# Delta rule of eight samples in a hybrid decoder step: the four heads of a group next to each other on TensorE

## The chip, the cores and the metric

The kernel is one launch on one NeuronCore of a Trainium2 chip. The metric is the device time of an execution in microseconds (us). Below, PE is TensorE, DVE VectorE, ACT ScalarE, POOL GpSimd, and SP the engine that only issues DMAs. A matmul of f32 data is two instructions in the trace, since the engine makes two passes over the moving operand; "pass" means one of these.

## The reference, cut to what matters

One layer of a decoder for a prompt of 512 tokens and for eight samples with one new token each: a modulated norm, an input projection, three branches (RG-LRU, gated DeltaNet, latent attention), their merge, and a feed forward part. What the change touches is the DeltaNet step of the samples. With T = 1 the chunked rule comes down, for each of 8 samples and 8 heads, to:

```python
kS = k @ S                      # S [128, 128], the state of this sample and head
U = beta * (v - exp(g) * kS)
o = exp(g) * (q @ S) + (q . k) * U
S_new = exp(g) * S + outer(k, U)
```

## The kernel before, in words

The kernel runs on one core, in stages: modulation and first norm, input projections with the prompt's delta rule, then a stage in which three things are interleaved (from about 490 to 745 us of the trace): the RG-LRU (`lru_steps`), the delta rule of the samples (`delta_samples`), and steps of the samples' latent attention (`sample_part`), which reads 32 pages of cache per sample. After it come the prompt's attention, the merge of the branches and the feed forward part. A loop over `lru_steps` draws one step of each other generator per turn; the instructions of a turn are then ordered per engine by a scheduler, from which each engine has one fixed list that it works off in order. So an instruction that waits holds up all that stand behind it on its engine.

The tile names that matter:

- `mm<-hh,whi`, `hl,whi`, `hh,wlo` (L170): the large products, each of three exact parts, with weights `raw` loaded from DRAM (L149, issued by ACT's queue), split into `whi` by ACT (L156) and `wlo` by DVE (L157).
- `s` (L871): the RG-LRU's gate products, of `xc` (a convolution, last step L376 on DVE) split into `xch` by ACT (L177) and `xcl` by DVE (L178).
- `sp<-cc,Qst` (L1090) and `sa<-cv,PT` (L1114): scores and weighted values of the latent attention of four samples. The stationary operand has 32 columns, and the outputs of the four samples lie on PSUM partitions 0, 32, 64 and 96, the four of them innermost in the loop. Their pages come by DMA, `cc` from SP (L1068) and POOL (L1063), `cv` from POOL (L1104).
- `St`: the states, eight tiles [128, 512] per group of four heads (four samples each), loaded by SP (L954), updated by DVE (L1011) and written back by SP (L1019).

`delta_samples` works on two groups t of four heads j. Per group PE computes into two PSUM tiles, `pK` and `pV`, with head j on partitions 32 j to 32 j + 7, one row per sample:

- `pK` (L964): for each head, for queries and keys (w = 0, 1), the sum over the samples s of a product whose stationary operand is `msk`, 8 columns of which all but column s are zero, and whose moving operand is the state of that sample and head, 128 columns. That is 64 matmuls, 128 passes, with the heads outermost: all 16 of head 0, then those of head 1, and so on.
- `pV` (L969 to L973): per head five small products that turn values, keys, q . k, exp(g) and -beta to rows per sample: two with 128 moving columns, three with one column.

Then ACT copies `pV` to `vt` (L976, L977), and DVE makes updates and outputs of `vt` and `pK` (L983 to L987). Before the groups, eight matmuls (L943), one per head, spread exp(g) over all partitions.

Of the kernel before, what the change touches and what calls it, by code (L numbers as in the profile page):

```python
# [20 lines left out]
T = 512  # L21
NS = 8
HB = 260          # columns of one half: 256 prompt tokens, then 4 samples
NT = 2 * HB
CW = 544          # columns after a convolution: 8 samples at 4s, prompt token t at 32 + t
# [7 lines left out]
# columns of the parameter array  # L33
# [8 lines left out]
# columns of the constant array  # L42
# [10 lines left out]
# gates whose product starts with the first tiles of the normalised input  # L53
EARLY = 2
# steps of the samples' attention per gate, block of the prompt's attention, part of a merge, step of the RG-LRU,
# block of values, pair of heads
STEPS = (1, 0.9, 1, 0.9, 0.5, 1.5)
# pages of a block of eight that GpSimd fetches; tiles of values
POOLED = (1, 3, 5)
VBUF = 5  # L60
# delta rule of the samples: its start among the steps of the RG-LRU; steps per gate there
DL = 8
GL = 5
# gates after each pair of heads of the delta rule, and before the first
# [7 lines left out]
def pr(t):  # L72
    """prompt columns of a [p, 520] tile"""
    return view2(t)[:, :, 0:256]


def sm(t):
    """sample columns of a [p, 520] tile"""
    return view2(t)[:, :, 256:260]


def csm(t):
    """sample columns of a [p, 544] tile as [p, 2, 4]"""
    return t[:, 0:32].rearrange("p (a b c) -> p a b c", a=2, b=4)[:, :, :, 0]


def cpr(t):
    """prompt columns of a [p, 544] tile as [p, 2, 256]"""
    return t[:, 32:544].rearrange("p (a b) -> p a b", a=2)
# [11 lines left out]
def emit(es, tc, I, O):  # L101
# [23 lines left out]
    e1 = C("eps")[:, 0:1]       # EPS  # L125
    e2 = C("eps")[:, 1:2]       # 4 EPS
    zero1 = C("eps")[:, 3:4]

    # banks of PSUM: the phase's pool, and how many buffers each tag has there
# [22 lines left out]
    def split(raw, n, p=wp, bufs=2):  # L152
        """exact sum of two float32r parts"""
# [9 lines left out]
    def gemm(pt, ws, xs, nk, k0=0, start=True, stop=True, halves=((0, 1),), ks=None):  # L163
        """pt [128, 2, 512] += W^T X over nk k-tiles; ws = (hi, lo), xs = lists (hi, lo) of tiles"""
# [16 lines left out]
    # ---------------------------------------------------------------- modulation and first norm  # L181
# [10 lines left out]
    def ada_a(i, p, bufs):  # L192
        """tiles i and 8 + i of 128 features of the modulation: four quarters of the product"""
# [12 lines left out]
    def ada_b(i, md):  # L206
        """their sum, features on partitions"""
# [6 lines left out]
    def ada_steps(p, bufs):  # L214
        """32 further tiles by eight: four at a time next to each other, two turned by one transposition"""
# [21 lines left out]
    def rstd_a(ss, n, a, p, tiles=None):  # L237
        """1 / sqrt(mean over n features + EPS) of half a from ss, sums of n / 128 squares; tokens on partitions"""
# [9 lines left out]
    def rstd_b(r, rs, pinned=False):  # L248
        """the same on all partitions (PSUM)"""
# [40 lines left out]
    # kept until the branches are merged  # L290
    ckv_s = cp.tile([128, 2, 8], F32, name="ckv_s")
    # latent and rotary rows of queries and new keys of the samples in three tiles of 96
    kns = cp.tile([96, 3, 8], F32, name="kns")
    Qst = cp.tile([96, 3, 8, 32], F32, name="Qst")         # sample, 8 heads and zeros
    G3 = cp.tile([128, 3, 8, 8], F32, name="G3")           # q, k, v of the samples (doubled)
    zz_s = cp.tile([128, 8, 8], F32, name="zz_s")          # z silu(z) of the samples (doubled)
    egS = cp.tile([8, 2, 8], F32, name="egS")              # exp(g), -beta of the samples: sample, head
    gng = cp.tile([128, 1], F32, name="gng")
    V.tensor_scalar(gng, Pm("gng"), 0.5, None, ALU.mult)
    osf = cp.tile([128, 8, 8], F32, name="osf")            # gated delta output of the samples  # L300
    omS = cp.tile([128, 8, 8], F32, name="omS")            # attention output of the samples
# [8 lines left out]
    with ExitStack() as pha:  # L310
# [51 lines left out]
        def conv(p, pt, state, w, bias, nb, y):  # L362
            """causal convolution of width 4 of [128, 2, 260] in PSUM; y: output [128, 544]"""
# [15 lines left out]
        with ExitStack() as sub:  # L379
# [8 lines left out]

            lc = cp.tile([128, 2, 10], F32, name="lc")    # -c/2, c/4 with c = 8 softplus(-lambda)
            R = pa.tile([8, 512], F32, name="R")          # g of the prompt, cumulated within chunks, by head  # L390
            gb = pa.tile([128, 4, 2, 8], F32, name="gb")  # the same and beta; tokens on partitions
            eg = pa.tile([128, 2, 4, 8], F32, name="eg")  # exp(g), -exp(g)

            # ------------------------------------------------------------ scalars of the gated delta rule, rotary key
            def softplus(x, t):
                """max(x, 0) + log1p(exp(-|x|)), log1p(y) = 2 atanh(y / (2 + y)); t: 3 scratch, out in t[2]"""
                V.tensor_scalar(t[0], x, -1.0, None, ALU.mult)
                V.tensor_tensor(t[0], t[0], x, ALU.min)                     # -|x|
                A.activation(t[0], t[0], AF.Exp)                            # y
                V.tensor_scalar(t[1], t[0], 2.0, None, ALU.add)  # L400
                V.reciprocal(t[1], t[1])
                V.tensor_tensor(t[1], t[1], t[0], ALU.mult)                 # z
                V.tensor_tensor(t[0], t[1], t[1], ALU.mult)                 # z^2
# [13 lines left out]
            # rotary key: rows 64-95 k cos, rows 96-127 swapped k sin, summed by a selection product  # L417
# [500 lines left out]
        def delta_samples(pz):  # L918
# [23 lines left out]
            for hd in range(8):  # L942
                TE.matmul(pe[:, hd * 8:hd * 8 + 8], egS[:, 0, hd:hd + 1].to_broadcast([8, 128]), ident[0:8, 0:8],  # L943
                          start=True, stop=True)
# [764 lines left out]
```

## Time and profile before

| what | us |
|---|---|
| median of 3 executions (lowest, highest) | 1605.75 (1605.42, 1611.96) |
| span of the profiled execution | 1588.3 |
| median less that span | 17.4 |
| PE busy in the span | 1506.9 (95%) |
| DVE, ACT, POOL busy | 823.2, 645.1, 241.5 |

The span runs from the first to the last instruction of the program in the one execution that was profiled. No device time is given for that execution alone; 17.4 us is what the median has beyond its span. Busy time counts an engine as busy while at least one of its instructions runs; on PE these overlap, so starts say more than lengths. The timeline merges neighbouring instructions of one kind (x125: that many), with the time from the first one's start to the last one's end; in brackets stand an engine's idle time before a row, and what ended it.

### The profile page before, as it was taken

What the parts mean: (1) busy time and instruction counts of PE and PEld (TensorE: products, weight loads), DVE (VectorE), ACT (ScalarE), POOL (GpSimd) and SP (SyncE); (2) the same over time, 40 slices, a digit from 0 to 9 for tenths busy, and PEclk for the clock granted to TensorE, in tenths of its full rate; (3) what the DMA queues carried; (4) which work ended last, traced back from release to release, by engine and by line L of the source; (5) the groups of instructions that cost most, each with busy time, mean ns of one, the idle gap of its engine ahead of it and who ended that gap; (6) DMA issues with size and microseconds to landing.
All of it is one profiled execution on the core that took longest, in us unless ns stands there. A gap on an engine that the chain in (4) does not pass through costs nothing. (4 is left out here: it accounts for less than half of the span.)

```text
span 1588.3 us, 33413 instructions
## 1 busy us (share of the span) xinstructions
PE 1506.9 (95%) x13302; PEld 1362.4 (86%) x13302; DVE 823.2 (52%) x1924; ACT 645.1 (41%) x1221; POOL 241.5 (15%) x391
## 2 busy tenths in 40 slices
PE   6899999999998999899889978999989999999997
PEld 4899999999897888688665567899979999999996
DVE  4587856847754675556354423354444333333334
ACT  4454645535434775455434423232234222222233
POOL 0121000101104441312224432000000000000001
PEclk9999999999998999999899989999999999999998
DMA  8233242342418973857777788576652222322232
GB/s 336 82 120 109 78 152 66 107 138 83 139 60 262 259 227 111 283 161 250 233 250 231 236 259 249 189 234 221 245 192 80 93 79 84 106 93 94 83 89 83
DMA packets 117774, 255.98 MB, mean 161 GB/s; under 512 B 22281, under 2 KB 53770, under 8 KB 117618
## 3 DMA queue, kind: packets, MB, share of 16 engines
q1 hardware_dynamic: 83904, 161.85, 31.7%
q0 software_dynamic: 13824, 47.72, 9.7%
q10 hardware_dynamic: 19890, 44.27, 8.5%
q8 instruction: 105, 1.72, 0.4%
q14 instruction: 51, 0.42, 0.1%
HBM read 228.61 MB, written 25.18 MB: 160 GB/s over the span
## 5 line engine op out<-in xcount | busy, mean ns | idle before, releaser
L156 ACT ACTIVATE whi<-raw 128x1024 fp32r<-128x1024 f32 (+3 forms) x208 | 202.7, 975 | 531.6 <-PE mm L170 478.6
L157 DVE TENSOR_TENSOR wlo<-raw,whi 128x1024 fp32r<-128x1024 f32 (+3 forms) x208 | 232.6, 1120 | 244.1 <-ACT whi L156 238.2
L170 PE MATMUL mm<-hh,whi 128*128 128x260 f32 x1312 | 280.4, 292 | 4.5 <-ACT hh L288 2.3
L170 PE MATMUL mm<-hl,whi 128*128 128x260 f32 x1312 | 274.4, 288 | 0.6 <-DVE hl L288 0.6
L170 PE MATMUL mm<-hh,wlo 128*128 128x260 f32 x1312 | 273.3, 287 | 0.5 <-DVE wlo L157 0.5
L170 PEld LDWEIGHTS mm<-hh,whi 128*128 128x128 f32 x1312 | 207.0, 191 | 14.5 <-issue 5.0
L170 PEld LDWEIGHTS mm<-hl,whi 128*128 128x128 f32 x1312 | 206.6, 191 | 4.7 <-issue 3.2
L170 PEld LDWEIGHTS mm<-hh,wlo 128*128 128x128 f32 x1312 | 205.7, 190 | 4.8 <-issue 2.8
L170 PE MATMUL mm<-h2h,wlo 128*128 128x260 f32 x704 | 142.0, 283 | 0.0
L170 PE MATMUL mm<-h2l,whi 128*128 128x260 f32 x704 | 141.7, 283 | 0.0
L170 PE MATMUL mm<-h2h,whi 128*128 128x260 f32 x704 | 141.3, 283 | 0.0
L170 PE MATMUL mm<-brh,whi 128*128 128x260 f32 x576 | 121.1, 289 | 10.5 <-ACT brh L177 5.8
L1063 POOL DMA_INDIRECT cc<-in_ckvT,pkx x96 | 99.1, 1032 | 132.9 <-PE sp L1090 90.6
L170 PE MATMUL mm<-brh,wlo 128*128 128x260 f32 x576 | 118.2, 286 | 0.9 <-DVE wlo L157 0.7
L170 PE MATMUL mm<-brl,whi 128*128 128x260 f32 x576 | 118.8, 286 | 0.2 <-DVE brl L178 0.2
L170 PEld LDWEIGHTS mm<-h2h,whi 128*128 128x128 f32 x704 | 108.2, 188 | 0.8 <-ACT h2h L288 0.4
L170 PEld LDWEIGHTS mm<-h2h,wlo 128*128 128x128 f32 x704 | 108.5, 188 | 0.4 <-DVE wlo L157 0.4
L170 PEld LDWEIGHTS mm<-h2l,whi 128*128 128x128 f32 x704 | 108.2, 188 | 0.4 <-DVE u L286 0.4
L170 PEld LDWEIGHTS mm<-brh,whi 128*128 128x128 f32 x576 | 90.3, 191 | 19.8 <-ACT whi L156 6.8
L170 PEld LDWEIGHTS mm<-brh,wlo 128*128 128x128 f32 x576 | 90.1, 190 | 1.6 <-DVE wlo L157 1.6
L170 PEld LDWEIGHTS mm<-brl,whi 128*128 128x128 f32 x576 | 90.1, 190 | 1.5 <-issue 0.8
L1497 POOL TENSOR_TENSOR x<-x,rf 128x260 f32<-128x260 f32 x6 | 5.4, 925 | 519.6 <-ACT rf L1491 519.6
(494 smaller groups left out, 2495.2 us busy)
## 6 DMA issues: line engine op xcount, KB each, us to landing
raw<-in_w_in SPq DMA_DIRECT2D x55, 512.0 KB, 3.6
wa<-in_w_ada SPq DMA_DIRECT2D x48, 512.0 KB, 4.3
cc<-in_ckvT SPq DMA_DIRECT2D x160, 144.0 KB, 5.6
raw<-in_w_f SPq DMA_DIRECT2D x44, 512.0 KB, 3.5
raw<-in_w_in ACTq DMA_DIRECT2D x27, 512.0 KB, 5.1
raw<-in_w_f SPq DMA_DIRECT2D x16, 384.0 KB
d_g<-gt ACTq DMA_DIRECT2D x22, 260.0 KB, 3.1
raw<-in_w_rg ACTq DMA_DIRECT2D x16, 320.0 KB, 2.9
```

The costliest lines, as they stand in the source:

```text
L156: A.activation(hi[:, :n], raw[:, :n], AF.Copy)
L157: V.tensor_tensor(lo[:, :n], raw[:, :n], hi[:, :n], ALU.subtract)
L170: TE.matmul(pt[:, a, 0:HB], w[:, k * 128:k * 128 + 128], x[k0 + k][:, a * HB:(a + 1) * HB], start=start and k == 0 and i == 0, stop=stop a ...
L1063: G.indirect_dma_start(ct[:, i].rearrange("p c t -> p (c t)"), None, I["ckvT"], bass.IndirectOffsetOnAxis(ap=pkx[0:96, o:o + 1], axis=0))
L1497: e.tensor_tensor(x1[k][:, sl], x1[k][:, sl], rs[a], ALU.mult)
```

## The change

It has three parts. In `pK` the loops are turned round, so that the four heads stand innermost. In `pV` likewise: each kind of product is made for the four heads in a row. And the eight matmuls that spread exp(g) become one: DVE multiplies exp(g) with a mask into `egd` [8, 64], a diagonal block of 8 for each head, and one product with ones gives the same 64 columns. Results, shapes and all later steps stay as they were. (The comments are also gone from the file.)

```diff
             pe = s_tile()
-            for hd in range(8):
-                TE.matmul(pe[:, hd * 8:hd * 8 + 8], egS[:, 0, hd:hd + 1].to_broadcast([8, 128]), ident[0:8, 0:8],
-                          start=True, stop=True)
+            egd = pz.tile([8, 8, 8], F32, name="egd")
+            V.tensor_tensor(egd, egS[:, 0].unsqueeze(2).to_broadcast([8, 8, 8]),
+                            ident[0:8, 0:8].unsqueeze(1).to_broadcast([8, 8, 8]), ALU.mult)
+            TE.matmul(pe[:, 0:64], ones[0:8, :], egd.rearrange("p h s -> p (h s)"), start=True, stop=True)
...
                 V.memset(pK[:, 0:256], 0.0)
                 V.memset(pV[:, 0:259], 0.0)
-                for j in range(4):
+                for w, s, j in product(range(2), range(8), range(4)):
                     hd = 4 * t + j
-                    for w in range(2):
-                        for s in range(8):
-                            TE.matmul(pK[32 * j:32 * j + 8, 128 * w:128 * w + 128],
-                                      msk[w][:, (hd * 8 + s) * 8:(hd * 8 + s) * 8 + 8],
-                                      St[2 * j + s // 4][:, (s % 4) * 128:(s % 4) * 128 + 128], start=s == 0, stop=s == 7)
-                for j in range(4):
-                    hd = 4 * t + j
-                    TE.matmul(pV[32 * j:32 * j + 8, 0:128], G3[:, 2, hd, :], ident, start=True, stop=True)
-                    TE.matmul(pV[32 * j:32 * j + 8, 128:256], qks[:, 1, hd, :], ident, start=True, stop=True)
-                    TE.matmul(pV[32 * j:32 * j + 8, 256:257], qks[:, 2, hd, :], ones[:, 0:1], start=True, stop=True)
-                    for w in range(2):
-                        TE.matmul(pV[32 * j:32 * j + 8, 257 + w:258 + w], ident[0:8, 0:8], egS[:, w, hd:hd + 1],
-                                  start=True, stop=True)
+                    TE.matmul(pK[32 * j:32 * j + 8, 128 * w:128 * w + 128],
+                              msk[w][:, (hd * 8 + s) * 8:(hd * 8 + s) * 8 + 8],
+                              St[2 * j + s // 4][:, (s % 4) * 128:(s % 4) * 128 + 128], start=s == 0, stop=s == 7)
+
+                for i, j in product(range(3), range(4)):
+                    a_ = (G3[:, 2], qks[:, 1], qks[:, 2])[i][:, 4 * t + j, :]
+                    n = 128 if i < 2 else 1
+                    TE.matmul(pV[32 * j:32 * j + 8, 128 * i:128 * i + n], a_, (ident if i < 2 else ones)[:, 0:n],
+                              start=True, stop=True)
+                for w, j in product(range(2), range(4)):
+                    TE.matmul(pV[32 * j:32 * j + 8, 257 + w:258 + w], ident[0:8, 0:8], egS[:, w, 4 * t + j:4 * t + j + 1],
+                              start=True, stop=True)
```

The scheduler also moves other instructions of this stage, between the spreading of exp(g) and about 745 us; before and after it the lists of the engines are the same.

On PE, the first group. `s<-St,msk` is `pK`; `s<-cst,G`, `s<-cst,qks` and `s<-egS,cst` are `pV`, four times the block shown here before the change:

```order
L170 MATMUL mm<-hh_101,wlo 128x260 x2
L964 MATMUL s<-St,msk 8x128 x64
L969 MATMUL s<-cst,G_77 8x128
L970 MATMUL s<-cst,qks 8x128
L971 MATMUL s<-cst,qks 8x1
L973 MATMUL s<-egS,cst 8x1 x2
...
L1090 MATMUL sp<-cc,Qst 32x256 x12
L170 MATMUL mm<-hh_94,whi 128x260 x2
```

and now:

```order
L170 MATMUL mm<-hh_101,wlo 128x260 x2
L963 MATMUL s<-St,msk 8x128 x64
L970 MATMUL s<-cst,G_77 8x128 x4
L970 MATMUL s<-cst,qks 8x128 x4
L970 MATMUL s<-cst,qks 8x1 x4
L973 MATMUL s<-egS,cst 8x1 x8
L1090 MATMUL sp<-cc,Qst 32x256 x12
L871 MATMUL s<-xch,rgwh 128x272
L871 MATMUL s<-xcl,rgwh 128x272
L871 MATMUL s<-xch,rgwl 128x272
```

The 64 matmuls of `pK` stay one run; `pV` goes by kinds; and a gate product of the RG-LRU (L871) now stands right behind the attention's scores, ahead of the large products.

On DVE, around the same group (L983 to L987 read `vt` and `pK`), before:

```order
L375 SCALAR_TENSOR_TENSOR cz<-cin,prm,xc 128x544
L376 SCALAR_TENSOR_TENSOR xc<-cin,prm,cz 128x544
L157 TENSOR_TENSOR wlo<-raw,whi 128x1024
L178 TENSOR_TENSOR xcl<-xc,xch 128x544
L983 COPY ku<-vt 128x128
L984 SCALAR_TENSOR_TENSOR ku<-s,vt 128x128
L986 TENSOR_SCALAR os<-s,vt 128x128
L985 TENSOR_SCALAR ku<-ku,vt 128x128
L1092 TENSOR_REDUCE mx<-sp 128x1
L987 SCALAR_TENSOR_TENSOR os<-ku,vt,os 128x128
L1095 TENSOR_REDUCE st<-mx 128x1
```

and now:

```order
L375 SCALAR_TENSOR_TENSOR cz<-cin,prm,xc 128x544
L157 TENSOR_TENSOR wlo<-raw,whi 128x1024
L376 SCALAR_TENSOR_TENSOR xc<-cin,prm,cz 128x544
L983 COPY ku<-vt 128x128
L984 SCALAR_TENSOR_TENSOR ku<-s,vt 128x128
L986 TENSOR_SCALAR os<-s,vt 128x128
L985 TENSOR_SCALAR ku<-ku,vt 128x128
L1092 TENSOR_REDUCE mx<-sp 128x1
L987 SCALAR_TENSOR_TENSOR os<-ku,vt,os 128x128
L1095 TENSOR_REDUCE st<-mx 128x1
L178 TENSOR_TENSOR xcl<-xc,xch 128x544
```

`wlo` moved ahead of the last step of the convolution, and `xcl`, which L871 reads, from ahead of the delta rule's steps to behind seven of them.

On ACT at the same place, before:

```order
L156 ACTIVATE whi<-raw 128x1024
L177 ACTIVATE xch<-xc 128x544
L976 ACTIVATE vt<-s 128x128
L977 ACTIVATE vt<-s 128x131
L149 DMA raw<-in_w_in 128x1024
```

and now:

```order
L156 ACTIVATE whi<-raw 128x1024
L976 ACTIVATE vt<-s 128x128
L977 ACTIVATE vt<-s 128x131
L149 DMA raw<-in_w_in 128x1024
L177 ACTIVATE xch<-xc 128x544
```

`xch` moved behind the copies of `pV` here. At the second group `xch` and `xcl` stand ahead of those steps, as before the change.

## Rows read from the trace of the kernel before

**Rows 1.** The page: the span, and the engines' busy time.

```profile
span 1588.3 us, 33413 instructions
PE 1506.9 (95%) x13302; PEld 1362.4 (86%) x13302; DVE 823.2 (52%) x1924; ACT 645.1 (41%) x1221; POOL 241.5 (15%) x391
```

**Rows 2.** Stretches of 40 us: busy us per engine, granted PE clock, DMA share, GB/s.

```profile
560.00:600.00 40.00, 39.93 (x375) 36.07 (x376) 27.12 (x49) 28.98 (x44) 15.80 (x20) 1.00 0.77 222
600.00:640.00 40.00, 39.33 (x374) 32.28 (x372) 24.05 (x54) 19.67 (x32) 9.52 (x14) 1.00 0.43 133
640.00:680.00 40.00, 34.59 (x293) 29.60 (x297) 23.49 (x51) 19.38 (x32) 11.57 (x14) 0.96 0.86 291
680.00:720.00 40.00, 39.53 (x404) 33.77 (x397) 21.94 (x45) 21.30 (x34) 9.46 (x12) 1.00 0.41 127
720.00:760.00 40.00, 36.42 (x313) 30.68 (x313) 23.11 (x56) 19.86 (x28) 12.62 (x14) 1.00 0.82 281
```

**Rows 3.** Timeline of PE, first group: start, us, engine, line, what, count.

```profile
601.30 12.53 PE L964 MATMUL s<-St,msk 128*8 128x128 f32 x125
...
613.67 0.27 PE L964 MATMUL s<-St,msk 128*8 128x128 f32 x1
613.68 0.27 PE L969 MATMUL s<-cst,G 128*8 128x128 f32 x1
613.78 0.27 PE L964 MATMUL s<-St,msk 128*8 128x128 f32 x1
...
614.00 0.19 PE L971 MATMUL s<-cst,qks 128*8 128x1 f32 x2
614.12 0.24 PE L973 MATMUL s<-egS,cst 8*8 8x1 f32 x4
614.30 0.39 PE L969 MATMUL s<-cst,G 128*8 128x128 f32 x2
...
616.49 1.50 PE L1090 MATMUL sp<-cc,Qst 96*32 96x256 f32 x24
```

**Rows 4.** The same for the second group.

```profile
687.12 12.53 PE L964 MATMUL s<-St,msk 128*8 128x128 f32 x125
...
702.31 1.50 PE L1090 MATMUL sp<-cc,Qst 96*32 96x256 f32 x24
```

**Rows 5.** The same, a run of the latent attention's weighted values.

```profile
630.44 1.93 PE L1114 MATMUL sa<-cv,PT 128*32 128x256 f32 x32
```

**Rows 6.** The same, where exp(g) is spread.

```profile
577.95 0.38 PE L926 MATMUL s<-jk,cst 128*128 128x128 f32 x2
578.27 1.95 PE L943 MATMUL s<-cst,egS 8*128 8x8 f32 x16
580.14 1.05 PE L1090 MATMUL sp<-cc,Qst 96*32 96x256 f32 x10
```

**Rows 7.** Timeline of ACT and DVE beside the first group, and DVE's `xcl` beside the second.

```profile
605.44 1.06 ACT L156 ACTIVATE whi<-raw 128x1024 fp32r<-128x1024 f32 x1 [1.99 <-DMA raw<-in_w_in]
616.60 0.28 ACT L976 ACTIVATE vt<-s 128x128 f32<-128x128 f32 x1 [9.56 <-PE s L973]
...
605.26 0.79 DVE L376 SCALAR_TENSOR_TENSOR xc<-cin,prm,cz 128x544 f32<-128x544 f32 x1
606.53 1.23 DVE L157 TENSOR_TENSOR wlo<-raw,whi 128x1024 fp32r<-128x1024 f32 x1 [0.48 <-ACT whi L156]
607.67 0.72 DVE L178 TENSOR_TENSOR xcl<-xc,xch 128x544 fp32r<-128x544 f32 x1
617.08 0.23 DVE L983 COPY ku<-vt 128x128 f32<-128x128 f32 x1 [8.69 <-ACT vt L977]
618.74 0.15 DVE L1095 TENSOR_REDUCE st<-mx 128x1 f32<-128x4 f32 x1
...
693.22 0.72 DVE L178 TENSOR_TENSOR xcl<-xc,xch 128x544 fp32r<-128x544 f32 x1 [0.72 <-ACT xch L177]
```

**Rows 8.** Timeline of PE after its longest wait of this stage.

```profile
675.21 0.59 PE L871 MATMUL s<-xch,rgwh 128*128 128x272 f32 x1 [4.33 <-ACT t L872]
```

**Rows 9.** Waits of SP's queue from 560 to 800 us: total, times, longest.

```profile
SPq L1019 <- DVE St L1011: 39.2, 11, 11.1
```

## The prediction

> **What bounds the kernel now.** I read the page first: PE is busy 1506.9 of 1588.3 us [rows 1], so time taken off PE's list is time off the kernel wherever PE does not wait. Then the stretches around the change, since the page's average says nothing of one stage. From 560 to 640 and from 680 to 720 us PE is busy 39.93, 39.33 and 39.53 of 40 us, at full clock; from 640 to 680 and from 720 to 760 it idles 5.41 and 3.58 us, and there the DMA share is 0.86 and 0.82 [rows 2]. The three places of the change, at 578, 601 to 616 and 687 to 702 us [rows 3, 4, 6], lie in the full stretches. There PE is the bound, and each microsecond saved is first of all kept.
>
> Third, PE's timeline. A group costs 15.19 us from its first pass to the first score pass behind it (601.30 to 616.49), and the second the same (687.12 to 702.31) [rows 3, 4]. The last passes of the fourth head show why: one pass of `pK` follows the one before it on the same head after 0.11 us (613.67, 613.78), but a pass of `pV` for the first head starts 0.01 us after the `pK` pass (613.68) [rows 3]. So passes that write the same 8 rows queue up at 0.11 us, and passes to another head's rows run beside them. With heads outermost nearly all passes are of the first kind: 128 times 0.11 is 14.1 us, less the little overlap where one head gives way to the next, and the row says 12.53.
>
> **The change, part by part.**
>
> *`pK`.* With heads innermost, four passes on four different row blocks stand together. The latent attention shows this already, with four samples innermost: its scores take 1.50 us for 24 passes [rows 3], its values, 128 rows deep like `pK`, 1.93 us for 32 [rows 5]. The difference, 0.43 us for eight passes, is two rounds of four: 0.22 us a round at 256 columns. For 128 columns that is half, 0.11 us, the same as one pass alone takes now: four for the price of one. 128 passes are 32 rounds, 3.5 us. The ends: no overlap at all leaves 12.53 us; I take 3.5, because rows 5 are the same shape but for the column count, and rows 3 show 8 column products already running side by side.
>
> The Trainium skill, page "TensorE: Matmul & The Clock Gate", section "Part 3: Packing small matmuls", gives 2.38 times for three column tiles instead of 3. Scaled to four (3.2 times, an estimate from that page) `pK` would take 4.4 us, and the whole 1.8 us more than my sum for both groups; rows 5 show no such loss, so the trace decides for the full factor.
>
> *`pV`.* Per group now 16 passes of 128 columns (four rounds, 0.44 us), 8 with one column and 16 with 8 rows and one column. The one column passes start about 0.03 us apart on the same rows (two in 0.19 us, four in 0.24) and 0.01 on others, so 0.06 and 0.11 us. Between the 128 row and the 8 row products PE pauses: from 614.00 to 614.12 and from 614.12 to 614.30 some 0.09 us are not explained by passes [rows 3]. Before there are eight such pauses per group, now two: 0.18 us. In all 0.8 us.
>
> So a group costs 3.5 + 0.8 = 4.3 us in place of 15.19, and two groups save **21.8 us**.
>
> *Spreading exp(g).* Now 1.87 us from its first pass to the next row (578.27 to 580.14). One matmul of 64 columns remains, two passes with a full 128 column stationary operand; the two such passes just ahead of it, with 128 columns, take 0.32 us (577.95 to 578.27) [rows 6]. Between 0 and 0.32 I take 0.32, and save **1.5 us**. Its new multiplication on DVE costs about what a small copy does, 0.23 us [rows 7]; it stands far ahead of its reader in DVE's list, and DVE idles 8.69 us at a stretch here, so it costs nothing; without that cover, 0.23.
>
> *What is late next.* The cover that goes is the group's own: 15 us in which ACT, DVE and the queues caught up. The copy of `pV` waited 9.56 us on ACT [rows 7], with the next weight load queued behind it; both now come 11 us sooner, which is a relief. But behind the group's 12 score matmuls (six rounds of 0.22, so at 4.3 + 1.3 = 5.6 us after the group's start) PE now has the RG-LRU's gate product, whose second matmul, wanted at about 5.8 us, reads `xcl`. First group: the convolution's last step ended 4.75 us after the group's start (605.26 + 0.79 - 601.30); `wlo` (1.23) has moved ahead of it, so 5.98; then DVE's steps from L983 to L1095 (617.08 to 618.89, 1.81) and `xcl` itself (0.72): 8.5 us, a wait of 2.7. The ends: nothing, if DVE gets there earlier, and 4.0, if `wlo` starts no sooner than its 606.53, since it waits for `whi`, and that for a DMA. Second group: `xcl` ended 693.94 [rows 7], 6.8 us after the start, a wait of 1.0, or nothing. All PE work, the large products above all, queues behind these two waits. I take **3.7 us** back.
>
> *Sum:* 21.8 + 1.5 - 3.7 = 19.6 us off a span of 1588.3. The median is 17.4 us above that span, which I carry over unchanged: 1605.75 - 19.6 = **1586.1 us**.
>
> **Rivals.**
>
> *The emptying takes over.* The four heads' results come sooner, but ACT and DVE are no faster, and weights and pages still come by DMA. PE's waits from 600 to 760 us are 10.1 us now (four times 40 us less what rows 2 give as busy). If the squeezed stage doubles them, the gain is 9.5 us: 1596.3. For it: DMA is at 0.86 and 0.82 of its time in the two stretches with waits, and one wait of 4.33 us for ACT stands in the first, after which PE's passes take 0.59 us with the granted clock at 0.96 for that stretch [rows 2, 8], so some of it ran at the half clock of 1.2 GHz. Against: from 600 to 640 and 680 to 720 us DMA is at 0.43 and 0.41, and that is the time being cut. The Trainium skill, page "TensorEngine Tiling (Array Packing)", section "PSUM Bottleneck", says just this: after a fourfold gain on TensorE the copy out of PSUM may become the bound. No row shows it here, since ACT waited for PE and not PE for the copy.
>
> *Nothing runs side by side.* If interleaved sums on four row blocks of one PSUM tile were not overlapped, only the spreading (1.5) and six pauses of 0.09 per group (1.1) would be saved: 1603.1, no change that can be told. Rows 3 and 5 speak against it.
>
> *Slower: SP's queue.* SP's write-backs of the states waited 39.2 us for DVE's updates, up to 11.1 at a time [rows 9], and the loads of pages for the next scores stand behind them in SP's list. Now this is hidden, since PE has other work meanwhile. If PE ran ahead so far that all of it came onto its path, the time would be 1605.75 - 19.6 + 39.2 = 1625.4. It decides from 27.6 of those 39.2 us on. Against: DVE's updates follow the groups' matmuls, so they start earlier too, and POOL loads a part of the pages past SP's queue.
>
> **How the numbers follow.** A measurement of this kernel can tell about 0.5%, 8 us, from no change. My forecast, a gain of 14 to 24 us, has 0.68. The emptying rival has 0.22, and most of it, 0.20, still counts as faster by over 8 us. No overlap has 0.06, the slower rival 0.04. That gives faster 0.88, same 0.08, slower 0.04. The range: without new waits the sum is 23.3 (1582.4), and if the 4.33 us wait went too, 1578.1; I begin between these at 1580. Above, the emptying rival's 1596.3 and the 1.3 us by which the first group's wait may be larger give 1597.6; I end at 1597.5.
>
> **What would show it.** Right: `pK` in about 3.5 us per group in rounds of four starts, group to scores 4.3 us, the spreading gone to 0.3; two waits of the gate product for `xcl`, 2.7 and 1.0 us; and from 760 us on all as before, some 20 us earlier. Wrong: `pK` rounds of 0.22 us or more (then the overlap was misread), PE idle of 20 us and more from 600 to 760 (then the emptying or the DMA is the bound), or waits of the scores for pages behind SP's write-backs.

## The result and the profile after

The changed kernel took a median of 1588.66 us (four runs, 1583.02 to 1592.83) against 1608.86 us of the kernel before beside it (four runs, 1605.42 to 1614.30): a ratio of 0.9891 with a 95% interval of [0.9855, 0.9926]. Two later measurements of the same file, each beside runs of the kernel before in the same session, gave 0.9866 [0.9832, 0.9900] and 0.9862 [0.9828, 0.9897]. It is faster by 1.1 to 1.4%.

The page of the changed kernel, the span and the engines' busy time, beside [rows 1]:

```profile
span 1590.1 us, 33384 instructions
PE 1500.7 (94%) x13288; PEld 1354.5 (85%) x13288; DVE 822.1 (52%) x1925; ACT 646.7 (41%) x1221; POOL 243.9 (15%) x391
```

This span is longer than that of [rows 1], in a kernel that is faster. Spans of two single executions can't be subtracted here: with the lists of the engines alike up to the change, PE reached L926 at 577.95 us in the execution of before [rows 6] and at 594.11 in that of after. So I compare the stage itself, from L926 to the first L1243, the first product of the stage that follows it. The windows view of exactly that stretch, first of before, then of after (length, busy us of PE, PEld, DVE, ACT, POOL, granted PE clock, DMA share, GB/s):

```profile
577.95:768.61 190.66, 178.90 (x1601) 149.63 (x1599) 107.79 (x231) 97.50 (x149) 50.15 (x62) 0.97 0.65 210
```

```profile
594.11:770.28 176.17, 159.89 (x1587) 133.35 (x1585) 107.36 (x230) 97.26 (x148) 52.19 (x62) 0.94 0.72 228
```

The stage is 14.5 us shorter. PE's busy time fell by 19.0, and its idle time (length less busy) rose from 11.76 to 16.28. Behind the stage these two executions are alike: 819.7 us from there to the end before, 819.8 after.

PE's timeline of after at the first group, beside [rows 3] (the second, from 695.12 to 699.39, is the same):

```profile
616.56 3.68 PE L963 MATMUL s<-St,msk 128*8 128x128 f32 x128
620.06 0.40 PE L970 MATMUL s<-cst,G 128*8 128x128 f32 x8
620.28 0.43 PE L970 MATMUL s<-cst,qks 128*8 128x128 f32 x16
620.64 0.26 PE L973 MATMUL s<-egS,cst 8*8 8x1 f32 x16
620.83 1.82 PE L1090 MATMUL sp<-cc,Qst 96*32 96x256 f32 x24
622.57 0.39 PE L871 MATMUL s<-xch,rgwh 128*128 128x272 f32 x1
622.80 0.29 PE L871 MATMUL s<-xcl,rgwh 128*128 128x272 f32 x1
```

`pK` takes 3.50 us to the first pass of `pV` (616.56 to 620.06), `pV` 0.77, and the group 4.27 (to 620.83) where it took 15.19. The spreading, beside [rows 6], takes 0.36 us from its first pass to the next row:

```profile
594.11 0.38 PE L926 MATMUL s<-jk,cst 128*128 128x128 f32 x2
594.43 0.43 PE L945 MATMUL s<-egd,cst 8*128 8x64 f32 x2
594.79 0.62 PE L1090 MATMUL sp<-cc,Qst 96*32 96x256 f32 x2
```

PE's list thus lost 2 x (15.19 - 4.27) + (1.87 - 0.36) = 23.35 us. A part of what was given back shows in PE's list of waits for the stage (what waited, for whom, us in total, times, longest), the largest of before, then of after:

```profile
PE s L871 <- ACT t L872: 4.3, 1, 4.3
PE sp L1090 <- ACT SC L1093: 4.3, 2, 3.3
```

```profile
PE s L871 <- ACT t L872: 6.8, 2, 6.3
PE sp L1090 <- ACT SC L1093: 3.7, 2, 2.8
PE sa L1114 <- ACT PT L1111: 1.7, 2, 1.0
```

The wait of L871 for ACT's `t` was there before [rows 8]; now it is longer. A turn has four such sums and two PSUM banks for them, so the third can start only when ACT has read the first. ACT's timeline of after ahead of that wait (rows with ACTq are transfers that ACT issues; in brackets the idle time before, and what ended it):

```profile
663.65 1.05 ACT L156 ACTIVATE whi<-raw 128x1024 fp32r<-128x1024 f32 x1
667.37 0.36 ACTq L358 DMA_DIRECT2D d_g<-gt  x1
669.24 4.76 ACTq L149 DMA_DIRECT2D raw<-in_w_in  x2
674.11 0.60 ACT L367 ACTIVATE cin<-mm 128x512 f32<-128x512 f32 x1 [9.41 <-DMA raw<-in_w_in]
677.12 1.06 ACT L156 ACTIVATE whi<-raw 128x1024 fp32r<-128x1024 f32 x1 [2.41 <-DMA raw<-in_w_in]
...
679.08 0.85 ACT L872 ACTIVATE t<-s,hb 128x272 f32<-128x272 f32 x2
```

`t` is ACT's reading of such a sum. ACT computes nothing from 664.70 to 674.11: a store (`d_g`) and two loads of weights stand there in its list and are issued only at 667.37 and from 669.24 on, and `cin`, `cz` and `t` stand behind them. The next section finds out which of this matters.

### The profile page after: what moved, and what is told of

It is laid out like the page before. It is cut to its first block, busy times and chain, and to the rows that moved or that the text cites. A ratio compares the mean times of both kernels' runs of the same rounds, so it can differ in the third digit from the quotient of the medians.

```text
span 1590.1 us, 33384 instructions
## 1 busy us (share of the span) xinstructions
PE 1500.7 (94%) x13288; PEld 1354.5 (85%) x13288; DVE 822.1 (52%) x1925; ACT 646.7 (41%) x1221; POOL 243.9 (15%) x391
## 5 line engine op out<-in xcount | busy, mean ns | idle before, releaser
L156 ACT ACTIVATE whi<-raw 128x1024 fp32r<-128x1024 f32 (+3 forms) x208 | 202.9, 977 | 515.9 <-PE mm L170 465.6
L170 PE MATMUL mm<-hh,whi 128*128 128x260 f32 x1312 | 281.7, 294 | 4.2 <-ACT hh L288 2.4
L170 PE MATMUL mm<-hl,whi 128*128 128x260 f32 x1312 | 276.9, 289 | 0.6 <-DVE hl L288 0.6
L170 PE MATMUL mm<-hh,wlo 128*128 128x260 f32 x1312 | 275.9, 289 | 0.5 <-DVE wlo L157 0.5
L170 PEld LDWEIGHTS mm<-hh,whi 128*128 128x128 f32 x1312 | 208.1, 193 | 14.9 <-issue 6.2
L170 PEld LDWEIGHTS mm<-hl,whi 128*128 128x128 f32 x1312 | 208.8, 192 | 5.5 <-issue 3.9
L170 PEld LDWEIGHTS mm<-hh,wlo 128*128 128x128 f32 x1312 | 208.0, 192 | 3.7 <-issue 2.4
L170 PE MATMUL mm<-h2h,wlo 128*128 128x260 f32 x704 | 142.0, 283 | 0.0
L170 PE MATMUL mm<-h2l,whi 128*128 128x260 f32 x704 | 141.7, 283 | 0.0
L170 PE MATMUL mm<-h2h,whi 128*128 128x260 f32 x704 | 141.3, 283 | 0.0
L170 PE MATMUL mm<-brh,whi 128*128 128x260 f32 x576 | 120.5, 288 | 4.2 <-ACT whi L156 2.9
L170 PE MATMUL mm<-brh,wlo 128*128 128x260 f32 x576 | 118.1, 285 | 0.9 <-DVE wlo L157 0.7
L170 PE MATMUL mm<-brl,whi 128*128 128x260 f32 x576 | 118.4, 285 | 0.0
L170 PEld LDWEIGHTS mm<-h2h,whi 128*128 128x128 f32 x704 | 108.2, 188 | 0.8 <-issue 0.8
L170 PEld LDWEIGHTS mm<-h2h,wlo 128*128 128x128 f32 x704 | 108.5, 188 | 0.4 <-DVE wlo L157 0.4
L170 PEld LDWEIGHTS mm<-h2l,whi 128*128 128x128 f32 x704 | 108.2, 188 | 0.4 <-DVE u L286 0.4
L170 PEld LDWEIGHTS mm<-brh,whi 128*128 128x128 f32 x576 | 89.9, 190 | 12.3 <-ACT whi L156 5.5
L170 PEld LDWEIGHTS mm<-brh,wlo 128*128 128x128 f32 x576 | 90.2, 190 | 1.6 <-DVE wlo L157 1.6
L170 PEld LDWEIGHTS mm<-brl,whi 128*128 128x128 f32 x576 | 89.8, 190 | 1.0 <-issue 0.8
L1090 PE MATMUL sp<-cc,Qst 96*32 96x256 f32 x768 | 73.2, 411 | 16.8 <-DMA cc<-in_ckvT,pkx 5.3
```

What stands on the lines that cost most here:

```text
L156: A.activation(hi[:, :n], raw[:, :n], AF.Copy)
L170: TE.matmul(pt[:, a, 0:HB], w[:, k * 128:k * 128 + 128], x[k0 + k][:, a * HB:(a + 1) * HB], start=start and k == 0 and i == 0, stop=stop a ...
L1090: TE.matmul(po[32 * j:32 * j + 32, 0:256], Qst[:, t, 4 * g + j, :], cts[j][:, :, t, :], start=t == 0, stop=t == 2)
```

## The experiments

All were timed in several rounds beside the kernel before. The ratio is to that. The stage runs from L926 to L1243 in the profiled execution, with PE's idle time in it, and the wait is that of L871 for `t` named above.

| kernel | ratio, 95% interval | stage us | idle us | wait us |
|---|---|---|---|---|
| before, profiled above | | 190.66 | 11.76 | 4.33 |
| before again | 0.9991 [0.9966, 1.0016] | 192.60 | 10.58 | 2.94 |
| the change, profiled above | 0.9891 [0.9855, 0.9926] | 176.17 | 16.28 | 6.30 |
| the change, second | 0.9866 [0.9832, 0.9900] | 173.38 | 14.87 | 6.61 |
| the change, third | 0.9862 [0.9828, 0.9897] | 176.72 | 17.48 | 7.99 |
| `pK` alone | 0.9899 [0.9866, 0.9931] | 175.10 | 11.65 | 3.95 |
| `pV` and spreading alone | 0.9988 [0.9962, 1.0015] | 191.96 | 15.04 | 7.46 |
| two heads side by side | 0.9902 [0.9871, 0.9934] | 180.36 | 14.65 | 7.10 |
| one head, two banks | 0.9984 [0.9957, 1.0012] | 190.61 | 13.94 | 5.24 |
| large product put back | 0.9813 [0.9783, 0.9844] | 169.31 | 11.27 | 1.83 |
| the same again | 0.9858 [0.9825, 0.9890] | 170.67 | 12.73 | 1.81 |
| ACT's copy behind `t` | 0.9837 [0.9803, 0.9871] | 176.87 | 16.94 | 8.40 |
| write-back left out | 0.9843 [0.9813, 0.9874] | 173.81 | 14.38 | 4.86 |
| ACT's loads behind `t` | 0.9855 [0.9805, 0.9904] | 174.81 | 14.71 | none |

**The two kernels unaltered**, to see what one execution can tell.

> The kernel before, once more, for a trace from the same session as the others. Theory 1 (the change takes time off PE's list, nothing else): median near 1606 to 1609 us, groups of 15.2 us from the first pass to the first score pass, as in the trace shown, and a span that is 1.7 us short of the device time. Rival (the trace shown is typical as it is, with 17 us of the median lying outside the span): the span again near 1588 while the median is near 1606.

> The changed kernel, once more. Theory 1: ratio 0.985 to 0.992 to the kernel before, groups of 4.3 us in the trace. Rival (the four runs of the result were lucky): ratio above 0.993.

> The changed kernel unaltered, as the comparison for the runs beside it. All theories: 0.985 to 0.991 of the kernel before; the wait of the gate products (L871) for ACT's t (L872) near 652 to 665 us of the span is 6 to 7 us.

Before again gave 0.9991, the change 0.9866 and 0.9862. The span of before again, 1588.2 us, is 1.8 short of the device time of that same execution, 1589.97, so its rival is out. Its median was 1592.26 and not 1606 to 1609, and that of the kernel before beside it 1590.63, where the other sessions had 1603.71 to 1608.86: the level differs between sessions, and only ratios taken side by side can be compared. With the executions shown above, the stage is 191.6 us on the mean of two before and 175.4 on the mean of three after: **16.2 us shorter**, PE's idle time 5.0 longer (11.2 to 16.2), its busy time 21.2 shorter. Single executions of one kernel differ by up to 3.3 us in the stage. The wait lay at 2.94 and 4.33 us before, at 6.30, 6.61 and 7.99 after, the last of them above the 6 to 7 us expected.

**`pK` alone.** From the kernel before; `pV` and the spreading stay.

```diff
-                for j in range(4):
+                for w, s, j in product(range(2), range(8), range(4)):
                     hd = 4 * t + j
-                    for w in range(2):
-                        for s in range(8):
-                            TE.matmul(pK[32 * j:32 * j + 8, 128 * w:128 * w + 128],
+                    TE.matmul(pK[32 * j:32 * j + 8, 128 * w:128 * w + 128],
```

> Only the states' products (pK) with heads innermost; the small products and the spreading as before. Theory 1 (each part gives what it takes off PE's list): a group's pK 3.5 us in place of 12.5, the gain 18 us of the whole change's 23, so 1588 to 1593 us beside 1606 to 1609 before. Rival (waits for weights eat the gain once PE runs ahead, the parts do not add): gain under 10 us.

PE's timeline of this run, first group:

```profile
606.63 3.68 PE L962 MATMUL s<-St,msk 128*8 128x128 f32 x128
610.13 0.38 PE L968 MATMUL s<-cst,G 128*8 128x128 f32 x2
...
613.06 1.50 PE L1089 MATMUL sp<-cc,Qst 96*32 96x256 f32 x24
```

`pK` takes the 3.50 us of the whole change, the group 6.43, so the list is 17.5 us shorter, and the stage is 16.5 us shorter. Here nearly all is kept. PE's idle time (11.65) and the wait (3.95) are those of before.

**`pV` and the spreading alone.** The change with `pK` as before.

```diff
-                for w, s, j in product(range(2), range(8), range(4)):
+                for j, w, s in product(range(4), range(2), range(8)):
                     hd = 4 * t + j
                     TE.matmul(pK[32 * j:32 * j + 8, 128 * w:128 * w + 128],
```

> Only the small products (pV) by kinds and the spreading in one product; pK as before. Theory 1: pV 0.8 in place of 2.6 us per group and the spreading 0.4 in place of 1.9, together 5 us less. Rival (the wait for weights behind the first group only gets longer): no gain, within 2 us of the kernel before.

The group takes 13.44 us, from the first row to the last of its timeline, and with the spreading the list is 2 x 1.75 + 1.51 = 5.0 us shorter:

```profile
612.38 12.53 PE L965 MATMUL s<-St,msk 128*8 128x128 f32 x125
...
625.82 1.77 PE L1091 MATMUL sp<-cc,Qst 96*32 96x256 f32 x24
```

Yet the stage is not shorter at all (191.96), with PE idle for 15.04 us, 3.9 more than before, and the longer wait:

```profile
685.59 0.59 PE L871 MATMUL s<-xch,rgwh 128*128 128x272 f32 x1 [7.46 <-ACT t L872]
```

So the longer wait goes with these two parts, not with the faster `pK`. What they have in common with the full change, and `pK` alone has not, is the order that the scheduler gave PE at this place. The windows view of the large products alone (L170), from the second gate product to the one that waits (length, busy us of PE and PEld with counts, clock, DMA), first of before, then of after:

```profile
667.00:675.20 8.20, 3.78 (x30) 3.67 (x30) 0.98 0.81 278
```

```profile
671.80:679.60 7.80, 1.48 (x11) 1.30 (x11) 0.74 0.94 325
```

Before, 30 of one large product's 48 matmuls stand ahead of the waiting L871, also with `pK` alone; after, 11, and as many with `pV` and the spreading alone. The other 19, worth 2.3 us, now stand behind it.

**Two heads side by side**, to measure what a round is.

```diff
-                for w, s, j in product(range(2), range(8), range(4)):
+                for h2, w, s, jj in product(range(2), range(2), range(8), range(2)):
+                    j = 2 * h2 + jj
```

> The changed kernel with two heads side by side instead of four (heads 0 and 1 first, then 2 and 3). Theory (rounds of as many products as there are different blocks of 32 rows and columns, some 0.11 us per round): pK takes 7.0 to 7.5 us per group instead of 3.5 to 3.7, the group 7.8 to 8.3 instead of 4.3; 3 to 8 us slower than the changed kernel, 0.988 to 0.992 of the kernel before. Rival (what counts is only that a product does not follow another into the same output): pK stays under 4 us, time as the changed kernel's, 0.985 to 0.988.

```profile
606.29 6.41 PE L964 MATMUL s<-St,msk 128*8 128x128 f32 x122
...
613.62 1.77 PE L1091 MATMUL sp<-cc,Qst 96*32 96x256 f32 x24
```

`pK` takes 6.4 us and the group 7.33 instead of 4.27, a little under the 7.0 to 7.5 and 7.8 to 8.3 expected. The first theory holds: `pK`'s time goes by rounds, and a round of two costs about what a round of four does. The two groups' 6.1 us stand beside 4.9 us of a longer stage than the change's mean of 175.4.

**One head, two banks**: heads outermost as before, but a head's queries and keys in turn go to two PSUM tiles, so that no product adds to what the one ahead of it wrote (the two passes of one product still go to the same place).

```diff
-                V.memset(pV[:, 0:259], 0.0)
-                for w, s, j in product(range(2), range(8), range(4)):
+                V.memset(pV, 0.0)
+                for j, s, w in product(range(4), range(8), range(2)):
                     hd = 4 * t + j
-                    TE.matmul(pK[32 * j:32 * j + 8, 128 * w:128 * w + 128],
+                    TE.matmul((pK[32 * j:32 * j + 8, 0:128], pV[32 * j:32 * j + 8, 384:512])[w],
...
-                V.scalar_tensor_tensor(Us, pK[:, 128:256], egc, vt[:, 0:128], ALU.mult, ALU.subtract)
+                V.scalar_tensor_tensor(Us, pV[:, 384:512], egc, vt[:, 0:128], ALU.mult, ALU.subtract)
```

> The changed kernel with the heads outermost again in pK, and each head's queries and keys in turn into two PSUM banks, so that no product follows another into the same output, while all of a head's stand on the same 8 columns of the array. Theory (only different blocks of the array run side by side): pK stays at 12 to 14 us per group, the group at 13 to 15; 0.995 to 1.000 of the kernel before. Rival (adding up in the same output is what keeps the products apart): pK 6 to 7.5 us per group, 0.988 to 0.992.

```profile
605.04 12.53 PE L963 MATMUL s<-St,msk 128*8 128x128 f32 x125
...
618.49 1.77 PE L1090 MATMUL sp<-cc,Qst 96*32 96x256 f32 x24
```

To the hundredth the 12.53 us of before [rows 3], and 0.9984 is close to the 0.9988 of the run with `pV` and the spreading alone, which has the same group but for the banks and the order within a head. If adding up in the same output kept products apart, half the time of `pK` should have gone. It goes by the head, that is by the block of output rows; what of all that belongs to a block (its rows, the place of its stationary operand) is the limit, these runs don't separate.

**The large product put back**, to test the order. The product of that turn is recorded ahead of the second half of the gate products (n is the step of the RG-LRU), and these are told to come behind its 30th matmul; the scheduler then put all 48 ahead.

```diff
                 for w in range(2):
+                    if w == 1 and n == 7:
+                        lru_g[n] = win_gemm(48 + n)
                     sl = slice(w * 128, w * 128 + 128)
...
-                            TE.matmul(pw[:, 0:272], a_[:, sl], b_[:, ca], start=i == 0, stop=i == 2)
+                            with tc.issue_after(mms[-19].ins) if w == 1 and n == 7 else nullcontext():
+                                TE.matmul(pw[:, 0:272], a_[:, sl], b_[:, ca], start=i == 0, stop=i == 2)
...
-                pt = win_gemm(48 + n)
+                pt = lru_g.pop(n) if n in lru_g else win_gemm(48 + n)
```

> The changed kernel, with one thing put back to about where it stood before: the large product of that turn (the one whose last 37 matmuls stood behind the waiting gate products) is placed ahead of them. Theory (order): the wait of L871 for ACT's t falls from 6 to 7 us to 2 us or less, because some 4.6 us of large products now lie ahead of it and nothing later waits in its place; 3 to 6 us faster than the changed kernel, 1568 or less where that is 1572. Rival (transfers): the engine waits as long, at this or the next large product, because the weights come no sooner; within 1 us of the changed kernel.

> The kernel with the large product placed back ahead of the waiting gate products, once more. Theory (order): 0.978 to 0.985 of the kernel before, and the wait of the gate products for t again under 2.5 us. Rival (the first measurement of it was a lucky one): 0.985 to 0.989, as the changed kernel.

The stage in the first run, and ACT and PE there:

```profile
584.19:753.50 169.31, 158.04 (x1587) 131.87 (x1586) 107.57 (x231) 97.10 (x149) 53.64 (x62) 0.96 0.74 234
```

```profile
664.47 0.60 ACT L369 ACTIVATE cin<-mm 128x512 f32<-128x512 f32 x1 [10.06 <-DMA St<-in_S]
```

```profile
669.31 0.40 PE L876 MATMUL s<-xch,rgwh 128*128 128x272 f32 x1 [1.83 <-ACT t L877]
```

ACT stands still as long as ever (10.06 us), but PE has work meanwhile: the wait is 1.83 us, and 1.81 in the second run. The stage is 169.31 and 170.67 us, 5.4 below the mean of the change and 21.6 below that of before, nearly all of the 23.35. The sums fit: 11, 30 and 48 matmuls keep PE busy for 1.32, 3.62 and 5.77 us, and with the waits behind them, 6.30, 4.33 and 1.83, that makes 7.62 (after), 7.95 (before) and 7.60 us (put back) from the second gate product to the third. `t` comes about as late in all three (over all runs with both loads ahead of it that sum lies between 6.2 and 9.3), and the wait is what the large product leaves of that time. In the stage the order is thus shown to be the cause of the longer wait. The whole kernel is a weaker witness: 0.9813 the first time, 9.6 us below the change timed beside it, where 3 to 6 were expected; 0.9858 the second time, as the change and as the rival had it. Of 5.4 us, 0.34%, such measurements can't be sure, so whether it beats the change by that much stays open.

**ACT's copy behind `t`.** The copy `whi` (L156) that waits 2.41 us in the rows of after is put behind the first two `t`.

```diff
-        A.activation(hi[:, :n], raw[:, :n], AF.Copy)
+        with tc.issue_after(tanh[-1].ins) if tanh else nullcontext():
+            A.activation(hi[:, :n], raw[:, :n], AF.Copy)
...
+                    tanh.extend(t0s if n == 8 else ())
                     lru_a(n + 1)
+                    tanh.clear()
```

> The changed kernel, with ACT's copy of the late weights (whi, L156) placed behind the two t of the gate products instead of ahead of them, and nothing else pinned. Theory (ACT's list holds up the gate products behind weights that come late): L871 waits under 1 us for t; the 42 large matmuls and 24 score matmuls that follow (some 6.8 us) cover the weights, whose large product waits under 1.5 us; 4 to 8 us faster than the changed kernel. Rival (the weights themselves bound it): the wait moves whole to the large product's first matmul (L170), 5 us or more; within 1.5 us of the changed kernel.

ACT in that run:

```profile
658.70 7.57 ACTq L149 DMA_DIRECT2D raw<-in_w_in  x2
666.37 0.60 ACT L370 ACTIVATE cin<-mm 128x512 f32<-128x512 f32 x1 [13.63 <-DMA raw<-in_w_in]
```

`t` no longer stands behind the copy and comes no sooner, so the wait is as long as ever, 8.40 us (only 6 matmuls stand ahead of it here), and does not move to the large product either; the stage is no shorter. (The median is 4.0 us below that of the change timed beside it, 1580.09 against 1584.05, but the intervals overlap, and the profile shows no place for it.) So both reasons fall for the wait: by its rows ACT stands at the issue of the two loads, which the last run below tests.

**The write-back left out.** The transfers in flight at that time are the states, pages and weights.

```diff
-                        out.append((O["gS_s"][hd, a], sx))
+                        if t:
+                            out.append((O["gS_s"][hd, a], sx))
```

> The changed kernel without the write-back of the first four heads' new states of the samples (eight transfers of L1019 left out, so these outputs stay unwritten). Theory (the transfers are full from 640 to 660 us, so the late weights come late because of the write-backs and loads of the states): the wait of L871 for t falls from 6 to 7 us to under 3 us and the time falls by 3 to 6 us against the changed kernel. Rival (the weights are late because they are issued late, behind a store in ACT's queue): the wait stays at 5 us or more, and the time within 1.5 us.

The wait became 4.86 us, the stage 173.81: between the two expectations. (The trace puts this wait down to the scores' `SC` ahead of `t` on ACT; but `SC` ends 0.43 us before L871 starts and the first `t` 0.05 us before, as in after, so it is `t` here too.) The whole kernel's 0.9843 lies inside the intervals of the change's second and third measurement, and the run with one head in two banks has 5.24 us with all write-backs in place. The write-backs have a share in the wait at most, and even that is not shown.

**ACT's loads behind `t`**, both loads and the copy.

```diff
-        queue[0].dma_start(raw[:, :n], src)
+        with late(0):
+            queue[0].dma_start(raw[:, :n], src)
...
-        A.activation(hi[:, :n], raw[:, :n], AF.Copy)
+        with late(1):
+            A.activation(hi[:, :n], raw[:, :n], AF.Copy)
```

(`late` holds an instruction behind the first or the second pair of `t` of that turn, for these two loads alone.)

> The changed kernel, with two loads of large weights (L149 on ACT's queue) and the copies of them taken behind the gate products' t of that turn, so that t and the convolution's cin ahead of it no longer stand behind them in ACT's list. The copies alone, moved in the run before, left cin idle for 13.6 us behind these loads. Theory (ACT itself stands still at the issue of a load until an earlier transfer has landed, and t stands behind it): the wait of L871 for t falls from 6 to 8 us to under 2 us; the weights come at most 3 us later and their large product waits under 3 us; 4 to 8 us faster than the changed kernel, 0.978 to 0.984 of the kernel before. Rival (t is late because its own inputs are, or the weights bound the place): the idle time moves whole to the next large product, 0.985 or more.

ACT in that run, then PE:

```profile
658.28 0.60 ACT L373 ACTIVATE cin<-mm 128x512 f32<-128x512 f32 x1 [5.32 <-PE mm L176]
...
660.26 0.85 ACT L878 ACTIVATE t<-s,hb 128x272 f32<-128x272 f32 x2
667.23 0.33 ACTq L154 DMA_DIRECT2D raw<-in_w_in  x1
667.67 0.42 ACT L183 ACTIVATE rgwh<-rgr 128x256 fp32r<-128x256 f32 x1 [6.56 <-DMA out_gS_s<-St]
```

```profile
671.87 0.80 PE L176 MATMUL mm<-hh,whi 128*128 128x260 f32 x2 [3.58 <-ACT whi L162]
...
690.41 0.60 PE L877 MATMUL s<-xch,rgwh 128*128 128x272 f32 x1 [3.92 <-ACT vt L987]
```

Now `t` is in time, at 660.26, and L871 doesn't wait for it: the loads' issue had held it. But the first load was still issued only at 667.23, and the trace names a write-back of the states as what ended ACT's idle time there; so PE waits for its weights instead, and later for `vt`, which stands behind the second load. The stage (174.81) and the idle time (14.71) hardly changed: the rival was nearer.

## Why the prediction was right, and where not

*`pK`, `pV`, the spreading: right.* 3.5 us forecast for `pK`, 3.50 measured; the group 4.3, measured 4.27 in both; the spreading 0.32, measured 0.36. The saving from the list, forecast as 21.8 + 1.5, was 23.35. The way it was read from [rows 3, 5], rounds of four at 0.11 us, held in two tests: rounds of two cost as much each, and passes of one head don't overlap even in two banks. The Trainium skill, page "TensorE: Matmul & The Clock Gate", section "Part 3: Packing small matmuls", gives 2.38 times for three column tiles; for four heads the prediction had estimated 3.2 times from it. Here 128 passes at 0.11 us alone would be 14.1 us and took 3.50, the full four times, so for these shapes the measurement decides against that estimate. What the page "TensorEngine Tiling (Array Packing)", section "PSUM Bottleneck", of the same skill warns of shows in after only as the 0.39 us wait below.

*The waits for `xcl`, 3.7 us: the step that failed.* In after, L871 ran through behind the first group with no wait; its product of `xcl` starts at 622.80 (rows above). DVE wrote the `xcl` that had moved only after that:

```profile
623.51 0.72 DVE L178 TENSOR_TENSOR xcl<-xc,xch 128x544 fp32r<-128x544 f32 x1
```

So it is another `xcl`. The tile has two buffers, and L871 reads that of the turn before; the names without buffer numbers read alike, and the two order listings from which the wait was worked out say nothing of which is which. At the second group PE waits 0.39 us, for ACT's reading of `pV` into `vt`, which frees the bank of PSUM, and not for `xcl`:

```profile
701.59 0.39 PE L871 MATMUL s<-xch,rgwh 128*128 128x272 f32 x1 [0.39 <-ACT vt L977]
```

*A wait that was not in the sum, and other idle time: +5.0 us.* The existing wait of [rows 8], 4.33 us, was in the prediction only as one that might go. On the means it grew from 3.6 to 7.0 us, 3.3 of the 5.0; the rest is spread over small waits. Of the 3.3, the 19 large matmuls that the scheduler moved from ahead of it account for 2.3; what remains is within the scatter of single executions. The order listings ahead of the prediction show the three places of the change, and this one lies between the groups. It is the kind of loss that the first rival named, at half of its price (5.0 of 10.1 us), though not from emptying that can't keep up: the place where ACT stands still is the same before and after, only PE's cover moved.

*Work of PE that got slower: +2.1 us.* PE's busy time fell by 21.2 us on the means, with 23.35 off its list. The scores of the latent attention grew by about as much. Their 24 passes behind a group took 1.50 us before [rows 3, 4] and take 1.82 in after (rows of the first group above). The windows view of the scores alone (L1090) over the stage gives 20.54 us of PE in before and 22.24 in after:

```profile
577.95:768.61 190.66, 20.54 (x236) 8.70 (x236) 0.97 0.65 210
```

```profile
594.11:770.28 176.17, 22.24 (x236) 9.09 (x236) 0.94 0.72 228
```

The other executions agree: 20.52 in before again, 22.23 and 22.86 in the second and third of the change. With `pK` alone it is 20.05, with `pV` and the spreading alone 22.20, so this loss, like the longer wait, goes with these two parts. Behind the first group four passes start within 0.02 us of 616.49 before, and the next four 0.24 us later. In after the first six start at 620.83, 620.89, 621.06, 621.07, 621.11 and 621.19, no longer in fours, though the samples stand in the same order in PE's list; why is open. The clock doesn't explain the 2.1 us: PE's work at half clock (granted clock 0.50) in the stage is 9.8 and 16.3 us in the two executions of before, and 13.4, 10.9 and 12.0 in the three of after.

*So the sum was right in part by luck: two errors cancel.* 3.7 us were taken off for waits that did not come, and 5.0 and 2.1 came elsewhere: 23.3 - 3.7 = 19.6 forecast, 23.35 - 7.1 = 16.2 measured in the stage. The ratios 0.9891, 0.9866 and 0.9862 mean 17.5 to 22 us of 1605, each within some 6 us either way, so whether the whole kernel gained 16.2 or 19.6 stays open.

*The 17.4 us "above the span": a wrong assumption without effect.* Time outside the span is 1.75 us (1591.85 of after against its span of 1590.1), and not 17.4. The profiled execution of before, 1588.3 us in span, was quicker than the four that were timed, of which the quickest took 1605.42. Executions differ ahead of the stage (PE reaches L926 between 577.29 and 594.11 us in those of the two kernels) and sessions differ in level, as said above; which of the two made these 16 us is not shown. Subtracting a saving from the median was right all the same, as the saving doesn't depend on it.

*The rivals.* Nothing side by side: refuted by the timeline. SP's queue: no; PE's waits for pages in the stage were 1.9 us before and 2.6 after, and from 560 to 800 us SP's waits at the write-backs (L1019) fell from 39.2 us [rows 9] to 21.1:

```profile
SPq L1019 <- DVE St L1011: 21.1, 11, 7.4
```

*What stays open:* why ACT's issues stand so long. The trace names transfers of SP's as what ended it (`St<-in_S`, `out_gS_s<-St`) and of ACT's own (`raw<-in_w_in`), by execution one or the other. Leaving out one set of write-backs took a part of the wait at most, and issuing the loads later moved it. Open, too, is why the scores got slower.

## What to carry to other kernels

Where small products write rows that lie 32 apart in the output, as the heads do here, write the loops so that neighbours go to different blocks: here 128 passes of 8 rows fell from 12.53 to 3.50 us for a reordering of loops, while sending a head's products to two banks in turn changed nothing. Then look at the whole stage's order, not only at the places of the change: a scheduler that is given other products may move the cover of an old wait, and here that and what came with it took back 7.1 of 23.35 us. And follow a tile by its buffer, not its name, before pricing a wait for it.

## What the runs showed of the hardware

- With the two loads of weights ahead in its list, ACT stood still for 8.7 to 13.6 us (`cin` [9.41 <-DMA raw], [13.63 <-DMA raw], [10.06 <-DMA St]) until, by the trace's releasers, a transfer, in some runs one of SP's queue, had landed. With the loads placed behind it `t` came at 660.26 and PE did not wait for it: a load on a computing engine's queue can hold up computing that has nothing to do with it.
- Passes of two heads in one round start 0.01 us apart and the next round 0.10 to 0.11 us later, with two heads as with four; passes of one head into two PSUM banks keep the 0.11 us each.
- The same list of instructions reached the stage as early as 577.29 us and as late as 594.11 in different executions (577.29 to 589.93 within one session), so single spans can't be compared to better than about 1%. In the two latest (589.93 and 594.11) the mean granted clock up to there was 0.97, in the others 0.98 or 0.99.
